# Ordering the second pair of adding transfers behind the last store in a two-branch encoder block

## The chip, the core and the metric

The kernel runs on one NeuronCore of a Trainium2 chip. The metric is the device time of one execution in microseconds (us), lower is better. Three runs of the kernel before gave 907.93, 908.09 and 908.94 us; the median is 908.09 us. The profile belongs to one further execution, of 908.01 us, on which all sums are made.

## The reference

One layer of an encoder block on x of 1024 tokens by 1024 channels, in float32. Cut to what matters here:

```python
h = rmsnorm(x, norm_g)
q, k, v, za, u, vs, zs, gm = split(h @ w_in)
a   = (window_sink_attention(rope(q), rope(k), v, sinks) * silu(za)) @ w_att_out
sgo = (gelu(u) * mix(layernorm(gelu(vs))) * silu(zs)) @ w_sg_out
ga, gs = split(sigmoid(gm + b_merge))
y = ga * a + gs * sgo
out = rmsnorm(x + y @ w_o, final_g)
```

The stretch of the kernel that the change touches begins with the product for za, goes on with the product of s = gelu(u) * mixed * silu(zs) with w_sg_out, and ends with the product of a (attention times silu(za)) with w_att_out.

## The kernel before

**Products.** Every large product is done as a seven-product (Strassen-like) scheme on halves. The right-hand side (the activations, 1024 channels by 1024 tokens) exists as seven "forms", named in the order in which the products use them: b11, t1, t2, b21, t3, b22, t4. Each form is 128 partitions by 4 by 512 numbers and is kept twice: a high part (fp32r, suffix h) and a low part, the rest (suffix l). The high part is a cast or a scaling on ScalarE (L154 for a form with changed sign, L159 without), the low part a subtraction on VectorE (L155, L160); each is made in two halves of 128x1024, so one form is four instructions. The weights (wh, wl) are split in the same two lines, in tiles of 128x1024 or 128x512.

`gemm_pair` (L359 and on) makes two row blocks of the result, with seven products of 12 matmuls each, in the order b11, t1, t2, b21, t3, b22, t4. Between them it empties the accumulators: x11 is copied after b11 (L368), x22 after t1 with changed sign (L372), x12 after t2 (L375), all on ScalarE; x11 += b21's product (L380), x22 -= the accumulator after t3 (L385) and x12 += b22's product (L389) on VectorE. Then `finish` is called for the four quarters in the order x11, x22, x12 and a fourth tile that takes t4's product, called the last quarter below. These x tiles share five buffers, which go round in the order of their first writing. So the copy of x22 in a pair reuses the buffer of x11 of the pair before, and the copy of x12 reuses that of x22: each has to wait until the store of that older tile has read it.

**Stages around the change.** Each stage is four calls of `gemm_pair`:

- The za stage: `finish` applies SiLU (L1670); a hook or more later the tile is multiplied by a tile of the attention result (`times`, L1557 or L1558) and stored to a_dr by a transfer that GpSimd issues (L466). The last pair's four stores are the end of the stage.
- The s stage (product with w_sg_out): `finish` multiplies by a gate (a sigmoid on ScalarE, L1683; the product on VectorE, L1692, or L1690 for the last quarter) and stores to y_dr, again by GpSimd (L466).
- The a stage (product with w_att_out): the same with the other gate, adding into y_dr.

**The forms of s and of a.** `forms_of` (L1510) makes the seven forms from four quarters of 128x4x512, called q11, q12, q22 and minus21, which lie in the four tiles bq0 to bq3. Its steps: q12 = q11 - q12 on VectorE; fill b11 from q11 and t1 from q12; q12 += q22 by a **first pair of adding transfers** (`add_aside`: two transfers of 128x2x512 issued by GpSimd, L202); fill b21 from minus21 and t2 from q12; minus21 += q12 by a **second pair of adding transfers**; q11 = q12 - q11 on VectorE (L190); fill t3 from q11 and b22 from q22. The form t4 is filled from minus21 after the second pair of adding transfers has landed. `last_form` asks for that at the third hook of the next stage's first pair, and its two casts are ordered behind the copy of x12 (`pace[0]`). The first steps happen while the stage before still runs its last pair.

**What sets the order.** Each engine works through its instructions in one order. A planner writes it before the run: it takes instructions by their place in the source as soon as it believes their operands to be ready. `after(second, first)` binds two instructions of one engine to an order without a wait for the first to finish. Transfers issued by GpSimd go through one software queue; those of SyncE (loads, L205) through another; all use the same 16 DMA engines. In what follows add2 means the second pair of adding transfers, with its two halves.

The order that GpSimd had before at the end of the za stage is: add1 first half, add1 second half, add2 first half, store of x11, add2 second half, stores of x22, x12 and the last quarter. At the end of the s stage: add1 (two), store of x11, add2 (two), stores of x22, x12 and the last quarter.

Of the kernel before, what the change touches and what calls it, by code (L numbers as in the profile page):

```python
# [27 lines left out]
ALU = mybir.AluOpType  # L28
# [24 lines left out]
def hybrid_tile(  # L53
# [16 lines left out]
    nc = tc.nc  # L70
# [91 lines left out]
    def after(second, first):  # L162

        tc.add_manual_dep(
            second.ins,
            first.ins.name,
            mybir.DependencyInfo(mybir.DependencyClass.NoSync, mybir.DependencyReason.DATA),
            reason="order",
        )
# [9 lines left out]
    def new_b(names=FORMS):  # L179
        return {n: (slot(n + "h"), slot(n + "l")) for n in names}  # L180

    def fill_b(b, name, src, minus=None):
        hi, lo = b[name]
        minus = name == "t2" if minus is None else minus
        return [
            split(hi[:, c : c + 2, :], lo[:, c : c + 2, :], src[:, c : c + 2, :], minus) for c in range(0, 4, 2)
        ]

    def combine(op, dst, a, c):
        return [op(dst[:, i : i + 2, :], a[:, i : i + 2, :], c[:, i : i + 2, :]) for i in range(0, 4, 2)]  # L190
# [8 lines left out]
    sums_to_make = []  # L199

    def add_to(dst, src):
        nc.gpsimd.dma_start(dst, src, accum_op=ALU.add)  # L202

    def copy_to(dst, src):
        nc.sync.dma_start(dst, src)  # L205
# [34 lines left out]
    def half_of(half):  # L240
        return slice(half * HALF, (half + 1) * HALF)
# [220 lines left out]
    def place(dst, m, half):  # L462
        return dst[m * P : (m + 1) * P, half_of(half)]

    def put(dst, m, half, src, queue=nc.sync):
        queue.dma_start(place(dst, m, half), src)  # L466

    def get(src, m, half, bufs, tag="g"):
        g = mtile([P, HALF], F32, tag, bufs, pool)
# [3 lines left out]
    def rest(dst, m):  # L473


        def finish(i, half, q, src, sign):
            if sign < 0:
                nc.scalar.mul(q[:], src, sign)
            put(dst, m + i, half, q[:])

        return finish
# [37 lines left out]
    for half in range(2):  # L519
        hi, lo = (part[:, half, :] for part in g_parts)  # L520
        src = g_row[:, half_of(half)]
# [40 lines left out]
    def add_on(dst, src):  # L562
        return nc.gpsimd.dma_start(dst, src, accum_op=ALU.add)
# [79 lines left out]
    def w_vs(i, j, c):  # L643
        return w[W_VS + 4 * i + 2 * j + c]

    def two_k(v, c):
        return v[:, 2 * c : 2 * c + 2, :]

    def flat(v):
        return v.rearrange("p k n -> p (k n)")  # L650
# [174 lines left out]
    for c in range(2):  # L825
        move = add_on(flat(two_k(raws["s3"], c)), w_vs(0, 0, c))
# [138 lines left out]
    def mix(g, half, q):  # L965

        pm = bank("tp")
        for t in range(4):
            nc.tensor.matmul(  # L969
                pm[:, t * P : (t + 1) * P],  # L970
                xh[:, half * 4 + t, g * P : (g + 1) * P],
                bias[-1][1][:, g % 4, :],
                start=True,
                stop=True,
            )
        p3 = pm[:].rearrange("p (t i) -> p t i", t=4)
        nc.vector.scalar_tensor_tensor(
            p3,
            p3,
            lg_sb[:, g : g + 1],  # L980
            bias[-1][0][:, g % 4, :].unsqueeze(1).broadcast_to([P, 4, P]),
            op0=ALU.mult,
            op1=ALU.add,
        )
        nc.vector.tensor_mul(q[:], q[:], pm[:])
        put(s1_dr, g, half, q[:])
# [198 lines left out]
    for m in range(0, KC, 2):  # L1185

        def finish(i, half, q, src, sign):
            if sign < 0:
                nc.scalar.mul(q[:], src, sign)
            put(q_raw, m + i, half, q[:])  # L1190
            rows = slice((m + i) * P, (m + i + 1) * P)
            split_q(q[:], [(slice(0, P), q_hl[:, rows, half_of(half)].rearrange("a p t -> p a t"))])

        if m == 2:
            steps_of_q.append(rope_tables())
        if m == 4:
            steps_of_q.append(rotate_keys(0))
            steps_of_q.append(rotate(0, 3))
        gemm_pair(hb, finish, part_of_q)
# [310 lines left out]
    def forms_of(qs, behind_t1=()):  # L1510
        q11, q12, minus21, q22 = (qs[k] for k in QUARTERS)
        b = {}

        def fill(name, q, minus=None):
            b.update(new_b((name,)))
            return fill_b(b, name, q, minus)

        def add_aside(dst, src):
            for i in range(0, 4, 2):
                add_to(dst[:, i : i + 2, :], src[:, i : i + 2, :])  # L1520

        combine(nc.vector.tensor_sub, q12, q11, q12)
        yield
        fill("b11", q11)
        low = fill("t1", q12)[-1]
        for move in behind_t1:
            after(move, low)
        add_aside(q12, q22)
        fill("b21", minus21, True)
        low = fill("t2", q12)[-1]  # L1530
        for hi in hi_of[-2:]:
            after(hi, of_units[-2])
        add_aside(minus21, q12)
        for sub in combine(nc.vector.tensor_sub, q11, q12, q11):
            after(sub, low)
        fill("t3", q11)
        fill("b22", q22)
        yield b
        fill("t4", minus21)
        for hi in hi_of[-2:]:  # L1540
            after(hi, pace[0])
        yield
# [118 lines left out]
    for m in range(0, KC, 2):  # L1661
        if m == 0:
            for _ in range(2):
                want_gate(at_dr, *of_att.pop(0))
        if m == 6:
            s_forms = forms_of(s_q, late_rows)
            next(s_forms)

        def finish(i, half, q, src, sign):
            pace[0] = nc.scalar.activation(q[:], src, AF.Silu, scale=sign)  # L1670
            silus.append((q, m + i, half))

        gemm_pair(hb, finish, lambda: part_of_s(m), "tp")
# [21 lines left out]
    for m in range(0, KC, 2):  # L1695
        if m == 2:
            a_q = {}
            ahead_of_time += loads_of_quarters(a_q, a_dr)
        if m == 6:
            a_forms = forms_of(a_q)  # L1700
            next(a_forms)

        def finish(i, half, q, src, sign):
            gated(q, src, sign, gate_of(gs_dr, m, i, half, KC))
            put(y_dr, m + i, half, q[:], nc.gpsimd)
            want_gate(*((gs_dr, m + 2 + i, half) if m < 6 else (ga_dr, i, half)))

        gemm_pair(sb_, finish, part_of_loads if m else last_form(s_forms, part_of_loads), "tp")
# [65 lines left out]
    for m in range(0, KC, 2):  # L1774
        if m == 6:
            written[0] += 1
            had = [mtile([P, D], F32, "s", 2) for _ in range(2)]
            for i in range(2):
                copy_to(had[i][:], y_dr[(m + i) * P : (m + i + 1) * P, :])

        def finish(i, half, q, src, sign):
            gated(q, src, sign, gate_of(ga_dr, m, i, half, 0))
            if m < 6:
                add_to(place(y_dr, m + i, half), q[:])
                want_gate(ga_dr, m + 2 + i, half)
            else:
                nc.vector.tensor_add(q[:], q[:], had[i][:, half_of(half)])
                if half == 1:
                    last_rows[i] = q
                copy_to(place(y_dr, m + i, half), q[:])  # L1790

        if m == 2:
            ahead_of_time += [lambda name=name: load_o(name, paced) for name in list(O_SOURCES)[:4]]
        hook = lambda: part_of_loads(3)
        gemm_pair(ab, finish, hook if m else last_form(a_forms, hook), "tp")
# [214 lines left out]
```

## Time and profile before

| what | value |
|---|---|
| median of three runs | 908.09 us |
| the profiled execution | 908.01 us |
| its span, first to last instruction | 906.2 us |
| busy time of TensorE (PE) | 893.7 us, 4290 matmuls |
| busy time of VectorE (DVE) | 690.1 us |
| busy time of ScalarE (ACT) | 530.0 us |
| busy time of GpSimd (POOL) | 149.9 us |
| software queue (issued by GpSimd) | 22464 packets, 62.93 MB |
| hardware queue (issued by SyncE) | 110072 packets, 149.74 MB |

A row of the timeline gives the start and the length in us, the engine, the line of the kernel, the operation, the tile written and the tiles read, the count, and in brackets how long the engine had been idle and what ended it. A row of the chain of waits gives start, length and what the time went to. A row of the windows view gives a stretch, its length, the busy time of each engine with its count of instructions, the granted share of the TensorE clock, the mean busy share of the 16 DMA engines and what they moved. GpSimd's rows for transfers are the time of issuing; the transfer itself ends at its landing, which the view of a tile gives as the time from issue to landing.

### The profile page before, as it was taken

The numbers are of one execution on the slowest core, as the hardware profiler recorded it, in microseconds if no ns is written. First come the engines' busy times: TensorE is split into PE (matmuls) and PEld (weight loads), VectorE is DVE, ScalarE is ACT, GpSimd is POOL, SyncE is SP. The second block draws the span as 40 slices with busy tenths as digits, with TensorE's granted clock in tenths as the row PEclk, the third lists the DMA queues.
The fourth block names the chain that finished last, engine by engine and source line by source line (L and its number), as shares of the span: only waits on it lengthen the run. The fifth ranks groups of instructions, "written<-read, shape, count | busy, mean of one in ns | idle before, by whom it ended". The sixth has DMA issues, their size and how long they took to land.

```text
span 906.2 us, 13224 instructions
## 1 busy us (share of the span) xinstructions
PE 893.7 (99%) x4290; PEld 746.1 (82%) x4290; DVE 690.1 (76%) x1256; ACT 530.0 (58%) x1061; POOL 149.9 (17%) x213
## 2 busy tenths in 40 slices
PE   9999999999999999999999999999999999999996
PEld 6888888888888888888888888888878887888885
DVE  6869966666686778887878888647796488479996
ACT  7866533334445567767677676664675375367443
POOL 2322222203030001111111011201111121110012
PEclk9999999999999999999999999999999999999999
DMA  9997888858778768788786779899899688998632
GB/s 330 208 256 209 263 204 178 169 155 267 254 247 296 209 179 216 209 178 204 171 229 220 241 233 239 211 329 356 310 284 378 220 235 240 305 292 269 208 118 114
DMA packets 132750, 213.77 MB, mean 236 GB/s; under 512 B 12777, under 2 KB 61161, under 8 KB 132682
## 3 DMA queue, kind: packets, MB, share of 16 engines
q1 hardware_dynamic: 110072, 149.74, 49.9%
q0 software_dynamic: 22464, 62.93, 31.1%
q8 instruction: 34, 0.56, 0.3%
q14 instruction: 34, 0.28, 0.1%
q10 hardware_dynamic: 146, 0.27, 0.1%
HBM read 147.74 MB, written 86.11 MB: 258 GB/s over the span
## 4 chain that ended last, share of the span: by engine, by line
PE 87%; issue 5%; DMA 5%; POOL 1%; DVE 1%; ACT 1%; POOLq 0%; DVEq 0%; ACTq 0%
PE ps_mm L350 36%; PE ps_o L350 27%; PE ps_sc L1294 3%; PE ps_mm L707 3%; PE ps_o L707 2%; PE ps_tp L707 2%; PE ps_o L1379 2%; PE ps_sc L350 2%; PE ps_tp L1338 2%; PE ps_tp L350 2%; DMA bq<-bq 2%; PE ps_tp L969 2%; DMA a_dr<-x 1%; PE ps_sc L707 1%; DMA y_dr<-x 1%
## 5 line engine op out<-in xcount | busy, mean ns | idle before, releaser
L159 ACT CAST wh<-s 128x1024 fp32r<-128x1024 f32 (+1 forms) x79 | 79.3, 1006 | 89.8 <-PE ps_mm L350 42.7
L160 DVE TENSOR_TENSOR wl<-wr,wh 128x512 fp32r<-128x512 f32 (+1 forms) x77 | 72.1, 938 | 53.2 <-ACT wh L159 52.2
L160 DVE TENSOR_TENSOR wl<-s,wh 128x1024 fp32r<-128x1024 f32 (+1 forms) x79 | 93.0, 1178 | 11.6 <-ACT wh L159 11.5
L159 ACT CAST wh<-wr 128x512 fp32r<-128x512 f32 (+1 forms) x77 | 63.1, 821 | 59.3 <-PE ps_mm L350 33.0
L350 PE MATMUL ps_o<-T_t1h,wh 128*128 128x512 f32 x148 | 58.6, 396 | 0.0
L350 PE MATMUL ps_mm<-T_t3h,wh 128*128 128x512 f32 x140 | 55.6, 397 | 2.8 <-ACT x L375 2.8
L350 PE MATMUL ps_o<-T_b22h,wh 128*128 128x512 f32 x148 | 58.3, 394 | 0.0
L350 PE MATMUL ps_o<-T_t1h,wl 128*128 128x512 f32 x148 | 57.8, 391 | 0.0
L350 PE MATMUL ps_o<-T_b22l,wh 128*128 128x512 f32 x148 | 57.8, 390 | 0.0
L350 PE MATMUL ps_o<-T_b22h,wl 128*128 128x512 f32 x148 | 57.7, 390 | 0.0
L350 PE MATMUL ps_o<-T_t1l,wh 128*128 128x512 f32 x148 | 57.6, 390 | 0.0
L1307 ACT ACTIVATE pr<-ps_sc,sm 128x192 f32<-128x192 f32 (+2 forms) x128 | 50.9, 410 | 8.8 <-DVE sm L1303 6.3
L350 PE MATMUL ps_mm<-T_t3h,wl 128*128 128x512 f32 x140 | 55.4, 395 | 0.0
L350 PE MATMUL ps_mm<-T_t3l,wh 128*128 128x512 f32 x140 | 55.2, 394 | 0.0
L350 PE MATMUL ps_mm<-T_t4h,wh 128*128 128x512 f32 x140 | 55.0, 393 | 0.0
L350 PE MATMUL ps_mm<-T_b11h,wh 128*128 128x512 f32 x140 | 54.9, 392 | 0.0
L350 PE MATMUL ps_mm<-T_t4h,wl 128*128 128x512 f32 x140 | 54.7, 391 | 0.0
L350 PE MATMUL ps_mm<-T_b11l,wh 128*128 128x512 f32 x140 | 54.7, 391 | 0.0
L350 PE MATMUL ps_mm<-T_b11h,wl 128*128 128x512 f32 x140 | 54.6, 390 | 0.0
L350 PE MATMUL ps_mm<-T_t2h,wl 128*128 128x512 f32 x140 | 54.6, 390 | 0.0
L350 PE MATMUL ps_mm<-T_t2h,wh 128*128 128x512 f32 x140 | 54.6, 390 | 0.0
L350 PE MATMUL ps_mm<-T_t2l,wh 128*128 128x512 f32 x140 | 54.6, 390 | 0.0
(399 smaller groups left out, 2402.6 us busy)
## 6 DMA issues: line engine op xcount, KB each, us to landing
wr<-in_w_dram SPq DMA_DIRECT2D x86, 256.0 KB
sums<-in_w_dram POOLq DMA_DIRECT2D x20, 512.0 KB, 6.7
s<-sums SPq DMA_DIRECT2D x20, 512.0 KB
q_hl<-qhl SPq DMA_DIRECT2D x16, 512.0 KB
q<-q_hl SPq DMA_DIRECT2D x64, 128.0 KB
y_dr<-x POOLq DMA_DIRECT2D x28, 256.0 KB, 6.8
g<-in_w_dram POOLq DMA_DIRECT2D x12, 512.0 KB, 7.0
wr<-in_w_dram SPq DMA_DIRECT2D x11, 512.0 KB
```

Of the source, the lines that this page charges most:

```text
L159: hi_of.append(nc.scalar.copy(hi, src))
L160: return nc.vector.tensor_sub(lo, src, hi.bitcast(F32))
L350: nc.tensor.matmul(acc, lt, rt, start=fresh and k == 0 and n == 0, stop=k == 3 and n == 2, skip_group_check=True,)
L707: mm = nc.tensor.matmul(acc[:], lt, rt, start=fresh and k == 0 and n == 0, stop=k == 3 and n == terms[-1], skip_group_check=True,)
L969: nc.tensor.matmul(pm[:, t * P : (t + 1) * P], xh[:, half * 4 + t, g * P : (g + 1) * P], bias[-1][1][:, g % 4, :], start=True, stop=True,)
L1294: nc.tensor.matmul(sc[:, i, k0:], q_of[:, c, i * P : (i + 1) * P], kt[:, f, k0:], start=f == 0, stop=f == 1,)
L1307: nc.scalar.activation(held_in[c, i], sc[:, i, lo:hi], AF.Exp, bias=nmax[:, c, i : i + 1], scale=-1.0, accum_out=sums[:, c, i : i + 1],)
L1338: nc.tensor.transpose(dst, pr[:, i, block * P : block * P + width], ident[:])
L1379: nc.tensor.matmul(po[:, cs], lt, rt, start=n == 0, stop=n == len(terms) - 1)
```

## The change

Every store made by `put` is recorded in a list. In `forms_of`, the two transfers of the second adding pair (minus21 += q12) are ordered on GpSimd behind the newest store in that list. For the forms of s that is the store of the last quarter of the za stage to a_dr; for the forms of a it is the store of the last quarter of the s stage to y_dr. Nothing is computed differently, and no other order is given.

```diff
     def add_to(dst, src):
-        nc.gpsimd.dma_start(dst, src, accum_op=ALU.add)
+        return nc.gpsimd.dma_start(dst, src, accum_op=ALU.add)
...
+    stores = []
+
     def put(dst, m, half, src, queue=nc.sync):
-        queue.dma_start(place(dst, m, half), src)
+        stores.append(queue.dma_start(place(dst, m, half), src))
...
         def add_aside(dst, src):
-            for i in range(0, 4, 2):
-                add_to(dst[:, i : i + 2, :], src[:, i : i + 2, :])
+            return [add_to(dst[:, i : i + 2, :], src[:, i : i + 2, :]) for i in range(0, 4, 2)]
...
-        add_aside(minus21, q12)
+        for move in add_aside(minus21, q12):
+            after(move, stores[-1])
         for sub in combine(nc.vector.tensor_sub, q11, q12, q11):
             after(sub, low)
```

## The prediction

> **What bounds the kernel now.** I read the page first, then the timeline of TensorE for gaps, then the chain of waits at each gap, and last the queues behind it.
>
> ```profile
> span 906.2 us, 13224 instructions
> PE 893.7 (99%) x4290; PEld 746.1 (82%) x4290; DVE 690.1 (76%) x1256; ACT 530.0 (58%) x1061; POOL 149.9 (17%) x213
> ```
>
> TensorE is the bound: an order on GpSimd can gain only where TensorE stands still. The timeline of TensorE shows two gaps around the change:
>
> ```profile
> 675.63 0.39 PE L350 MATMUL ps_tp<-T_b21h,wl 128*128 128x512 f32 x1
> 678.28 0.50 PE L350 MATMUL ps_mm<-T_t3h,wh 128*128 128x512 f32 x1 [2.26 <-ACT x L375]
> ...
> 685.47 0.39 PE L350 MATMUL ps_mm<-T_b11h,wh 128*128 128x512 f32 x1
> ...
> 686.60 0.39 PE L350 MATMUL ps_mm<-T_t4h,wh 128*128 128x512 f32 x1
> ...
> 755.96 0.39 PE L350 MATMUL ps_tp<-T_b21h,wl 128*128 128x512 f32 x1
> 756.92 0.50 PE L350 MATMUL ps_mm<-T_t3h,wh 128*128 128x512 f32 x1 [0.57 <-ACT x L375]
> ...
> 763.62 0.39 PE L350 MATMUL ps_mm<-T_t4h,wh 128*128 128x512 f32 x1
> ```
>
> Both stand at the same place: in the first pair of the s stage and of the a stage, ahead of t3, which needs the accumulator that the copy of x12 (L375) empties. Note the order: after t3 and b22 come five matmuls of the next pair's b11 (685.47), and only then t4 (686.60). The chain of waits says what the copy waited for:
>
> ```profile
> 665.90 11.66 DMA a_dr<-x
> ...
> 677.64 0.59 ACT x L375
> ...
> 678.28 4.60 PE ps_mm L350 x12
> ...
> 745.96 10.24 DMA y_dr<-x
> ...
> 762.65 5.44 PE ps_mm L350 x24
> ```
>
> It waited for the store of the old x22, whose buffer it reuses. That store took 11.66 us in one stage, 10.24 in the other. The last row is the undisturbed pace: 24 matmuls in 5.44 us, 2.72 a product. The t3 product at 678.28 took 4.60. The windows view says why, and how full the transfers are:
>
> ```profile
> 675.20:678.60 3.40, 1.14 (x5) 0.65 (x4) 2.40 (x3) 0.96 (x2) 0.00 (x0) 1.00 0.96 377
> 678.60:682.00 3.40, 3.40 (x10) 2.62 (x9) 2.80 (x3) 3.37 (x4) 0.00 (x0) 0.51 0.73 240
> 660.00:679.00 19.00, 16.74 (x73) 13.54 (x72) 17.13 (x19) 12.66 (x17) 3.94 (x6) 0.99 1.02 302
> 741.00:757.00 16.00, 15.43 (x69) 12.48 (x67) 16.00 (x18) 10.22 (x13) 3.35 (x5) 1.00 1.04 296
> ```
>
> After a stretch of 3.4 us in which TensorE was busy for 1.14, its granted clock was 0.51 for the next 3.4 us. And the 16 DMA engines were fully busy (shares 1.02 and 1.04) over the whole time in which stores and adding transfers were under way.
>
> **What goes: the two gaps.** Without its wait, t3 would start 0.23 us after the last matmul of b21, at 675.86, and t4 5.44 + 5 x 0.227 = 6.57 later, at 682.43; it started at 686.60. That is **4.17 us**, 2.4 of standing still and 1.8 of the half clock. In the a stage: 755.96 + 0.23 + 6.57 = 762.76 against 763.62, **0.86 us**. Together 5.03 us, if nothing else is late. Does the wait go? GpSimd's issues, in order:
>
> ```profile
> 655.80 0.87 POOL L202 DMA_DIRECT2D bq<-bq  x1 [0.25 <-DMA g<-at_dr]
> 660.99 0.85 POOL L202 DMA_DIRECT2D bq<-bq  x1 [4.32 <-DVE x L385]
> 661.74 0.68 POOL L466 DMA_DIRECT2D a_dr<-x  x1
> 665.35 0.85 POOL L202 DMA_DIRECT2D bq<-bq  x1 [2.94 <-DVE wl L160]
> 665.90 1.42 POOL L466 DMA_DIRECT2D a_dr<-x  x2
> 667.56 0.55 POOL L466 DMA_DIRECT2D a_dr<-x  x1 [0.23 <-DVE x L1557]
> 685.25 0.54 POOL L466 DMA_DIRECT2D y_dr<-x  x1 [17.14 <-DVE x L1692]
> ...
> 745.42 0.85 POOL L202 DMA_DIRECT2D bq<-bq  x1 [3.15 <-DVE wl L160]
> 745.96 1.96 POOL L466 DMA_DIRECT2D y_dr<-x  x3
> ```
>
> The second half of add2 (665.35) stands on GpSimd ahead of three stores, and both halves are ahead of them in the queue. With the change the store of x22 is issued before 665.35 and has only the store of x11 and the first adding pair ahead in the queue. In the view of the tile: the landings of that pair (issued at 654.67 and 655.80); those of the last store of the za stage (667.56) and of the last two of the s stage (the second and third of the three at 745.96, the third issued at 747.1); and that of the adding transfer that took least, with nothing ahead of it (issued at 735.00):
>
> ```profile
> DMA to landing us min/median/max: 5.8/7.4/9.0
> ```
>
> ```profile
> DMA to landing us min/median/max: 11.7/11.7/11.7
> ...
> DMA to landing us min/median/max: 10.8/11.0/11.1
> ```
>
> ```profile
> DMA to landing us min/median/max: 5.4/5.4/5.4
> ```
>
> The first adding pair is through at 655.80 + 9.0 = 664.8. Behind it the store of x22, half the size of the transfer that took 5.4 us alone, is down by 665.35 + 5.4 = 670.8, and t3 wants its accumulator only at 675.86: the copy of x12 no longer waits. I count the 5.03 us as won at that place.
>
> **What is added: add2 becomes last in the queue.** Its halves are issued after the last store, at 667.56 + 0.55 = 668.1 and about 669.0. Behind them GpSimd was idle for 17.14 us, until the first store of the s stage (685.25), so their wait blocks no issue there. Their landing is the unknown cost. Lower end: nothing in front, 669.0 + 5.4 = 674.4. Upper end: the longest time in the rows, 669.0 + 11.7 = 680.7. I take **679.8**, near the upper end, because of the queue's order and not of a typical time: the six transfers (two adding halves, four stores) are the same and go through in order, the engines were full, and the last of them landed at 667.56 + 11.7 = 679.2. Whichever is last lands about then; now it is the second half of add2, which before was ahead of three stores. To that comes up to 1.3 us in which the queue waits for the last products, half of it counted. In the a stage the last landing was 11.1 us after an issue at 747.1, which is 758.2, and I take **758.9** (758.2 to 759.5).
>
> **Who waits for add2.** Form t4: its casts, and on the in-order engines everything written behind them. ScalarE first, then VectorE:
>
> ```profile
> 678.12 1.99 ACT L159 CAST T_t4h<-bq 128x1024 fp32r<-128x1024 f32 x2
> 680.13 1.28 ACT L1683 ACT_TABLE_LOAD   x1
> 681.43 0.72 ACT L1683 ACTIVATE g<-g,bm_sb 128x512 f32<-128x512 f32 x1
> 682.06 1.03 ACT L159 CAST wh<-wr 128x1024 fp32r<-128x1024 f32 x1
> ...
> 756.76 2.00 ACT L159 CAST T_t4h<-bq 128x1024 fp32r<-128x1024 f32 x2
> ```
>
> ```profile
> 683.12 1.23 DVE L160 TENSOR_TENSOR wl<-wr,wh 128x1024 fp32r<-128x1024 f32 x1 [0.96 <-ACT wh L159]
> 684.87 0.68 DVE L385 TENSOR_TENSOR x<-x,ps_mm 128x512 f32<-128x512 f32 x1
> ...
> 690.93 1.22 DVE L190 TENSOR_TENSOR bq<-bq,bq 128x1024 f32<-128x1024 f32 x1 [2.24 <-DMA bq<-a_dr]
> ...
> 762.45 0.68 DVE L385 TENSOR_TENSOR x<-x,ps_mm 128x512 f32<-128x512 f32 x1
> ```
>
> Behind the second cast of t4 on ScalarE come the table load, the first gate and the cast of the next pair's weights, which its b11 needs; on VectorE behind t4's low parts comes L385, which frees the accumulator that t4 adds into. From the start of the second t4 cast (678.12 + 0.95 = 679.07) to the end of L385 (685.55) went 6.48 us, and t4 started 1.05 later. In the a stage the same is 757.71 to 763.13, 5.42 us. These chains have no idle time worth naming but that for one another, so I move them whole with the landing.
>
> - s stage: second cast at 679.85, L385 done 6.48 later, hand-over 0.1: t4 at 686.43 against 686.60. Of 4.17 us won, 4.0 are given back; 0.17 is left.
> - The half clock: the next weights' cast ends 4.02 us after the second t4 cast starts, at 683.9, the low part at 685.1. TensorE has finished b22 at 681.30 and stands until 683.9, so from 682.0 to 685.4 it is busy for some 0.8 us, less than the 1.14 after which the clock was halved. Of the next 3.4 us t4 gets about 2.4 at half pace: 1.2 lost. Its bounds: 0 and 1.8, which it cost before.
> - a stage: second cast at 758.95, 5.42 and 0.1 later t4 at 764.47 against 763.62: 0.85 us later than before. There TensorE waits only some 1.1 us for the low part of the weights, so no half clock.
>
> The Trainium skill ("TensorE: Matmul & The Clock Gate", section "HAM oscillation — how this bites in real kernels") puts the rule as no idle gaps above about 3.4 us; this case's trace speaks against it, since a gap of 2.4 us brought the half clock. By that rule the new gap would cost nothing more and the sum would be 1.2 us less.
>
> SyncE's first load of a quarter of a goes into the buffer that add2 reads, so it also waits for the landing, 1.5 us longer than before; behind it are two more loads of a. Their reader, L190 at 690.93, already stands 2.24 us, and the work behind it is for t3 of the next pair, 8 us later: counted at nothing; without that cover it would cost up to 1.5.
>
> **The sum.** 908.01 - 0.17 + 1.2 + 0.85 = 909.9, say **910.0 us**. The profiled execution stands 0.1 under the median of the runs, 908.09. With the landings 0.6 us sooner in both stages and no half clock it is 907.5; with 0.7 later, and the half clock at its bound, 912.
>
> **Rivals.**
>
> *The adding transfers land early.* If an adding transfer is held up only by its own length, its 5.4 us decide: landing at 674.4 and, in the a stage, by 755, both before the copy of x12 would have ended. Then t4's casts follow the copy as now and the full 5.03 us are won: **903.0 us**. For it: 5.4 and 5.8 us were seen. Against it: both were at the head of an empty queue, and the DMA share was above 1. It decides from a landing before about 676, each us later giving back one. The Trainium skill ("DMA: Bandwidth & Descriptors", section "Anatomy of one DMA — SWDGE (gpsimd) path") fits such a transfer at 2.0 us plus its bytes over 436 GB/s, an estimate of 3.2 us for 512 KB; by it this rival would hold. The rows above, 5.4 us at best, do not agree.
>
> *The planner turns the order around.* If it believes add2 to land later than the gate's inputs, it writes table load, gate and weight cast ahead of t4's casts. Then nothing but t4 itself waits: its second half needs a cast of 1.04 and a low part of 1.23 us after the landing, so is ready at 682.1, and would be wanted at 682.43 + 1.36. Also **903.0 us**. Against it: before, it held add1 landed within some 6 us (issued to 655.80, add2's first half put at 660.99, ahead of the store of x11), and from 669.0 add2 has as long until the copy of x12. The trace cannot show this order.
>
> *Later still.* Quarters of a, gates and weights load through the same full engines. If the landing slips to 682 and 761, the slip (2.2 and 2.1 us) counts in full, and the half clock goes on: **914 us**. Against it: the bytes ahead of add2 in its own queue are the same as before.
>
> *No effect.* The order of GpSimd's issues is exactly what is bound, so the change does what it says; 908.0 could only come out as a balance.
>
> **How the numbers follow.** Forecast 0.58, the two early cases together 0.27, later still 0.15. About 0.2% (1.8 us) is what a measurement of this kernel can tell from no change. The forecast's own range, 907.5 to 912, lies on both sides of 909.8: 0.35 slower, 0.20 the same, 0.03 faster. Later still is slower; of the early cases 0.26 faster, 0.01 the same. So faster 0.29, same 0.21, slower 0.50. The range for 8 in 10 runs from 902.9, which takes in the early cases, to 912.5.
>
> **What would show it.** In the profile after: GpSimd issues four stores in a row and then both halves of add2; no gap ahead of t3 in either first pair, and the copy of x12 waiting for nothing; instead a gap ahead of the next pair's b11 near 681.3 to 684, ended by the weight cast at L159; t4's second cast starting at a landing near 680 and 759; a stretch at half clock near 685. It is wrong if add2 lands before 677, or if the gate at L1683 stands ahead of t4's casts on ScalarE.

## The result, and the profile after

The kernel after takes 912.92 us (median of six runs, 912.37 to 914.85), against 908.01 us for six runs of the kernel before beside them (905.47 to 908.94). The ratio on record is 1.0075, with a 95% interval of 1.0060 to 1.0091: slower by about 0.75%. The quotient of these two medians is smaller, 1.0054, below that interval; a second measurement (after again, below) gave 1.0081, and 1.0084 by the medians. The forecast was 910.0 us with a range to 912.5. The direction was right, the size too small, and the time lies 0.4 us outside the range. The profiled execution took 912.37 us:

```profile
span 910.6 us, 13223 instructions
```

The timeline of GpSimd shows the order that was meant: four stores, then both halves of add2, and in the a stage the same.

```profile
661.57 0.57 POOL L468 DMA_DIRECT2D a_dr<-x  x1 [5.05 <-DVE x L1559]
...
667.40 0.54 POOL L468 DMA_DIRECT2D a_dr<-x  x1 [1.20 <-DVE x L1559]
668.02 1.79 POOL L202 DMA_DIRECT2D bq<-bq  x2
...
748.30 1.14 POOL L468 DMA_DIRECT2D y_dr<-x  x2 [1.77 <-DVE x L1694]
749.50 1.78 POOL L202 DMA_DIRECT2D bq<-bq  x2
```

The timeline of ScalarE shows what came of it, first for the s stage, then for the a stage:

```profile
673.51 0.58 ACT L375 COPY x<-ps_mm 128x512 f32<-128x512 f32 x1
677.11 1.05 ACT L159 CAST T_t4h<-bq 128x1024 fp32r<-128x1024 f32 x1 [3.02 <-DMA bq<-bq]
680.33 1.05 ACT L159 CAST T_t4h<-bq 128x1024 fp32r<-128x1024 f32 x1 [2.17 <-DMA bq<-bq]
...
683.31 1.03 ACT L159 CAST wh<-wr 128x1024 fp32r<-128x1024 f32 x1
...
759.37 1.05 ACT L159 CAST T_t4h<-bq 128x1024 fp32r<-128x1024 f32 x1 [2.57 <-DMA bq<-bq]
762.67 1.05 ACT L159 CAST T_t4h<-bq 128x1024 fp32r<-128x1024 f32 x1 [2.25 <-DMA bq<-bq]
```

The copy of x12 (L375) has no bracket any more: it waits for nothing. The wait now stands in front of the two casts of t4, and its releaser is add2. The next pair's weights are cast only at 683.31, behind t4's second cast, the table load and a gate. The timeline of TensorE follows:

```profile
675.69 0.39 PE L350 MATMUL ps_mm<-T_t3h,wh 128*128 128x512 f32 x1
...
684.39 0.79 PE L350 MATMUL ps_mm<-T_b11h,wh 128*128 128x512 f32 x1 [3.10 <-ACT wh L159]
...
687.10 0.63 PE L350 MATMUL ps_mm<-T_t4h,wh 128*128 128x512 f32 x1
...
691.51 0.39 PE L350 MATMUL ps_mm<-T_b11h,wl 128*128 128x512 f32 x1
...
693.12 0.39 PE L350 MATMUL ps_o<-T_t1h,wh 128*128 128x512 f32 x1
...
758.40 0.39 PE L350 MATMUL ps_mm<-T_t3h,wh 128*128 128x512 f32 x1
...
765.33 0.50 PE L350 MATMUL ps_mm<-T_b11h,wh 128*128 128x512 f32 x1 [1.33 <-ACT wh L159]
...
767.96 0.50 PE L350 MATMUL ps_mm<-T_t4h,wh 128*128 128x512 f32 x1 [0.23 <-DVE x L385]
...
772.41 0.39 PE L350 MATMUL ps_o<-T_t1h,wh 128*128 128x512 f32 x1
```

The gap ahead of t3 is gone in both stages. The new gap stands ahead of the next pair's b11, 3.10 us in the s stage, and t4's twelve matmuls take 691.51 - 687.10 = 4.41 us. The windows view of the same stretch (busy times of the engines, then granted clock, share of the transfer engines and GB/s) says why:

```profile
680.42:683.83 3.41, 0.87 (x4) 0.38 (x2) 1.82 (x2) 3.38 (x4) 0.00 (x0) 1.00 0.68 181
683.83:687.24 3.41, 2.80 (x6) 1.72 (x7) 2.87 (x4) 3.30 (x5) 0.58 (x1) 0.50 1.05 397
687.24:690.65 3.41, 3.41 (x10) 2.64 (x9) 2.50 (x4) 0.00 (x0) 1.09 (x2) 0.50 0.97 333
```

The clock stood at one half for 6.8 us, twice the stretch that was forecast.

**One measure for both stages.** From t3 of the first pair to t1 of the second stand 48 matmuls (t3, b22, t4 and the next b11), 48 x 0.2267 = 10.88 us at full pace. What lies above that is the loss of a stage; where t3 itself waits, the count begins at the end of b21. The kernel before had t1 here:

```profile
690.91 0.39 PE L350 MATMUL ps_o<-T_t1h,wh 128*128 128x512 f32 x1
...
767.93 0.39 PE L350 MATMUL ps_o<-T_t1h,wh 128*128 128x512 f32 x1
```

Before: 690.91 - 675.86 - 10.88 = 4.17 us lost in the s stage and 767.93 - 756.19 - 10.88 = 0.86 in the a stage. After: 693.12 - 675.69 - 10.88 = 6.55 and 772.41 - 758.40 - 10.88 = 3.13. The sum went from 5.03 to 9.68, up by 4.65, and the profiled execution from 908.01 to 912.37, up by 4.36. So, to within 0.3 us, the whole of the difference lies in these two places.

All kernels by this measure (us; the losses come from each one's profiled execution; medians of 4 to 12 runs, one for the last row; in the two kernels with the gap filled, the loss in s includes the 5.9 us of the filling matmuls):

| kernel | lost in s | lost in a | profiled | median | ratio to before (95%) |
|---|---|---|---|---|---|
| before | 4.17 | 0.86 | 908.01 | 908.01 | |
| after | 6.55 | 3.13 | 912.37 | 912.92 | 1.0075 (1.0060 to 1.0091) |
| order in the s stage alone | 6.26 | 0.97 | 908.66 | 909.10 | 1.0040 (1.0025 to 1.0055) |
| order in the a stage alone | 0.94 | 3.39 | 907.24 | 908.94 | 1.0028 (1.0012 to 1.0044) |
| behind the store of x22 | 1.59 | 0.00 | 904.76 | 905.29 | 0.9987 (0.9976 to 0.9999) |
| after, weights early | 4.21 | 2.54 | 910.42 | 910.10 | 1.0047 (1.0031 to 1.0063) |
| before, weights early | 0.63 | 0.88 | 904.39 | 906.68 | 1.0009 (0.9994 to 1.0024) |
| after, fewer loads | 1.88 | 0.00 | 904.41 | 905.61 | 1.0003 (0.9991 to 1.0014) |
| after, gap filled | 5.90 | 4.34 | 920.89 | 920.83 | 1.0175 (1.0157 to 1.0193) |
| after, gap filled, second try | 6.04 | 3.46 | 910.28 | 912.94 | 1.0070 (1.0044 to 1.0096) |
| behind x22, weights early | 0.13 | 0.13 | 903.17 | 903.28 | 0.9973 (0.9960 to 0.9987) |
| after again | 6.53 | 3.37 | 913.11 | 913.21 | 1.0081 (1.0057 to 1.0105) |
| before again | 3.18 | 0.98 | 907.26 | 907.26 | |

Beside the later kernels the kernel before had medians of 906.08, 905.58 and 905.59 us (31, 29 and 11 runs, 902.88 to 909.28 in all). So ratios are compared below, not times.

### The profile page after: what moved, and what is told of

It is laid out like the page before. It is cut to its first block, busy times and chain, and to the rows that moved or that the text cites. A ratio compares the mean times of both kernels' runs of the same rounds, so it can differ in the third digit from the quotient of the medians.

```text
span 910.6 us, 13223 instructions
## 1 busy us (share of the span) xinstructions
PE 895.5 (98%) x4290; PEld 745.8 (82%) x4290; DVE 689.8 (76%) x1256; ACT 529.6 (58%) x1061; POOL 149.8 (16%) x213
## 4 chain that ended last, share of the span: by engine, by line
PE 77%; issue 13%; DMA 5%; POOL 2%; ACT 1%; DVE 1%; SPq 0%; POOLq 0%; ACTq 0%; DVEq 0%
PE ps_mm L350 31%; PE ps_o L350 24%; PE ps_sc L1296 3%; DMA bq<-bq 3%; PE ps_mm L709 2%; PE ps_o L709 2%; PE ps_tp L709 2%; PE ps_sc L350 2%; PE ps_o L1381 2%; PE ps_tp L1340 2%; PE ps_tp L971 2%; PE ps_sc L709 1%; DMA g<-at_dr 1%; PE ps_sc L593 1%; PE ps_tp L350 1%
## 5 line engine op out<-in xcount | busy, mean ns | idle before, releaser
L350 PE MATMUL ps_mm<-T_t4l,wh 128*128 128x512 f32 x140 | 55.2, 395 | 0.0
```

What stands on the lines that cost most here:

```text
L350: nc.tensor.matmul(acc, lt, rt, start=fresh and k == 0 and n == 0, stop=k == 3 and n == 2, skip_group_check=True,)
```

## The experiments

**Each stage alone.** One of the two calls gets the order of before.

```diff
-    def forms_of(qs, behind_t1=()):
+    def forms_of(qs, behind_t1=(), bound=True):
...
         for move in add_aside(minus21, q12):
-            after(move, stores[-1])
+            if bound:
+                after(move, stores[-1])
...
-            a_forms = forms_of(a_q)
+            a_forms = forms_of(a_q, bound=False)
```

The other kernel has `bound=False` in the call for the forms of s.

> The order stands for the forms of s alone; those of a have the order of before. If each stage pays for its own wait (the chain behind t4's casts moves with the landing of add2), the time is that of before plus what t4 lost in the s stage, 693.12 - 690.91 = 2.2 us: 908.0 + 2.2 = 910.2 us, the stretch of 6.8 us at half clock after 683.8 is there again, and the a stage has its gap ahead of t3 back. Rival: the s stage's loss is won back by slack later on, and the whole change comes from the a stage: 908.0.

> The order stands for the forms of a alone. If each stage pays for its own wait, the time is 908.0 + 2.3 = 910.3 us (the a stage's part of the 4.48 us by which the next pair's t1 came later in the kernel after), with the gap of 2.3 us and the half clock of before in the s stage, and the second half of add2 landing some 2.3 us later against the last products than the queue's end did before. Rival: 908.0, or 912.4 if it is the a stage alone.

Each is slower by itself, by 0.40% and 0.28%; the sum, 0.68%, lies within the interval of both together. Each stage pays for itself. One part of the first expectation missed: with the order in the s stage alone the half clock lasted 3.41 us (684.55 to 687.96) and not 6.8, although the gap ahead of b11 was longer, 3.64 us. The kernel with the order in the a stage alone showed something else in the s stage, where it has the order of before. Its ScalarE there:

```profile
675.34 0.59 ACT L375 COPY x<-ps_mm 128x512 f32<-128x512 f32 x1 [1.21 <-DMA a_dr<-x]
```

The store of the old x22 let the copy go at 675.34, where the profile of before had 677.64, and t3 hardly waited (0.05 us): this execution lost 0.94 us in the s stage, not 4.17.

**Before and after once more.** The same two kernels again.

> The kernel after once more, beside the kernel before on the same chip. If the losses of the two stages add up, the ratio is that of the order in the s stage alone plus that in the a stage alone, 1.0040 + 0.0028: 1.007, and the trace again has t1 of the second pair 17.4 us behind t3 in the s stage and 14.0 in the a stage (10.9 without a wait). If they don't, the ratio is nearer to one of the two alone, 1.003 to 1.004.

> The kernel before once more. The first profile of it had lost 4.2 us in the s stage (t3 to the next t1 15.1 us from the end of b21, against 10.9 without a wait), 1.8 of them to the half clock. If that is what every execution loses, it is seen again. If the wait for the store varies from execution to execution and passes into the half clock only where it is long, as the s stage of the kernel with the order in the a stage alone suggests (0.9 us lost, no half clock), this one may show less, and its time then is lower by the same amount: 905 us with a loss of 1 us.

After again has a ratio of 1.0081, losses of 6.53 and 3.37, and so adds up as expected. Before again lost 3.18 us in the s stage, with nearly the wait of the first profile and yet without the half clock (0.9 of the 3.18 lie behind t3, where b11 and t4 wait). TensorE, and the windows view:

```profile
678.09 0.50 PE L350 MATMUL ps_mm<-T_t3h,wh 128*128 128x512 f32 x1 [2.13 <-ACT x L375]
```

```profile
673.40:676.81 3.41, 2.56 (x12) 1.79 (x10) 3.41 (x4) 0.99 (x2) 0.00 (x0) 1.00 1.01 365
676.81:680.22 3.41, 2.13 (x9) 1.79 (x10) 1.46 (x3) 2.75 (x4) 0.00 (x0) 1.00 0.66 210
```

The boundaries of the two stretches are the times at which this trace's own clock can change (the last section says how that is read from the traces). The wait lies across such a boundary, so that TensorE was busy for 2.56 and 2.13 us of 3.41; in the first profile nearly the same wait lay within one stretch, of which 1.14 us were busy, and the half clock followed.

So what the kernel before loses in the s stage differs from execution to execution (4.17, 3.18, 0.94 and 0.63 us in four profiles that have its order there), by the landing of one store and by whether the half clock follows. The loss in the a stage hardly differs (0.86 to 0.98).

**What stands behind t4's casts.** The next pair's weights are split ahead of t4's casts and of the gates, in the first pair of both stages.

```diff
         pace[0] = nc.scalar.copy(x12[:], acc)
         split_next()
+        if soon:
+            split_next()
         hook()
...
         finish(0, 0, x11, x11[:], 1.0)
-        split_next()
+        if not soon:
+            split_next()
...
             after(hi, pace[0])
+            after(hi, of_units[-1])
...
         after(gate, pace[0])
+        if m == 0:
+            after(gate, of_units[-1])
```

> The change as it is, and in the first pair of the s and of the a stage the next pair's weights are cast and split ahead of t4's casts and ahead of the gates. Nothing is taken from add2's wait. Theory (the loss comes from what is queued behind t4's casts on ScalarE and VectorE, not from t4 itself): next b11 follows b22 without a gap, no half clock in the s stage, and t4 starts when the second low part (landing + 1.05 + 1.23) and L385 (0.7 more) are done, near 683.4 in place of 687.1 and about 765.7 in place of 768.0: 912.4 - 3.7 - 1.7 - 2.3 = 904.7 us. Rival (the landing of add2 itself is what t4 waits for, with the rest hidden): 911 to 912.5 us.

> The kernel before, with the next pair's weights cast and split ahead of t4's casts and of the gates in the first pair of the s and the a stage. Theory (in the kernel before, the copy of x12 is what TensorE waits for, and t4's casts are off the path): same as the kernel before within 0.5 us. Rival (the chain behind t4's casts costs time in the kernel before too): 2 us faster.

On the kernel before it changes nothing that can be told (1.0009, with 1 in the interval). On the kernel after it takes the ratio from 1.0075 to 1.0047, 2.5 us and not the 7.7 expected. ScalarE, VectorE and TensorE of that kernel, and two windows of each stage:

```profile
676.21 1.06 ACT L159 CAST wh<-wr 128x1024 fp32r<-128x1024 f32 x1 [1.57 <-PE ps_tp L350]
...
680.96 1.05 ACT L159 CAST T_t4h<-bq 128x1024 fp32r<-128x1024 f32 x1 [2.24 <-DMA bq<-bq]
```

```profile
682.04 1.23 DVE L160 TENSOR_TENSOR T_t4l<-bq,T_t4h 128x1024 fp32r<-128x1024 f32 x1 [2.07 <-ACT T_t4h L159]
...
683.78 0.68 DVE L388 TENSOR_TENSOR x<-x,ps_mm 128x512 f32<-128x512 f32 x1
```

```profile
684.60 0.47 PE L350 MATMUL ps_mm<-T_t4h,wh 128*128 128x512 f32 x1 [2.31 <-DVE x L388]
...
764.95 0.47 PE L350 MATMUL ps_mm<-T_t4h,wh 128*128 128x512 f32 x1 [2.29 <-DVE x L388]
```

```profile
681.95:685.36 3.41, 1.10 (x5) 0.67 (x4) 3.32 (x5) 3.38 (x6) 0.00 (x0) 1.00 0.96 292
685.36:688.77 3.41, 3.41 (x9) 2.65 (x8) 2.71 (x4) 1.47 (x2) 1.54 (x3) 0.50 1.05 373
...
760.46:763.87 3.41, 2.20 (x10) 1.50 (x8) 1.49 (x2) 2.57 (x4) 0.00 (x0) 1.00 0.58 204
763.87:767.28 3.41, 2.33 (x10) 1.99 (x11) 3.41 (x6) 1.89 (x3) 1.58 (x2) 1.00 0.20 70
```

The theory holds for the weights: they are cast at 676.21, and the gap ahead of b11 is gone. But t4 itself still waits, 2.3 us in each stage, for L385 (here L388), which stands with L380 (here L382) behind t4's low parts on VectorE. The chain from the landing to t4 became 684.60 - 680.96 = 3.64 us in place of 687.10 - 680.33 = 6.77. The wait passes into the half clock in the s stage (685.36) and not in the a stage, and the planner now puts two matmuls of b11 ahead of t4 where five stood, which takes 0.7 us of cover away in each stage. So both theories were partly right: the chain shrank by nearly half, but of the 9.68 us lost only 2.9 went (6.75 are left), and for the rest t4 still waits on the landing.

**The half clock.** 26 matmuls into a bank that nobody reads fill the gap of the s stage.

```diff
         product(t5, ready[n, 5], b["b22"], False)
+        if idle:
+            spare = bank("sc")[:]
+            for i in range(idle):
+                nc.tensor.matmul(spare, ready[n, 5][0][:, 0:P], b["b22"][0][:, 0, :], ...)
```

> The change as it is, with 26 matmuls of 128x512 into a spare bank behind b22 of the s stage's first pair (5.9 us of work that nobody reads), so that TensorE is busy until t4 is ready at 687.1. The five matmuls of the next b11 then come behind t4 and not ahead of it. Theory (half of what the s stage lost behind t4's start is the half clock, 1.7 us): no half clock after 683.8, t4's product takes 2.72 us and not 4.41, and the next t1 starts at 687.1 + 5.44 = 692.6, 0.5 us sooner than after although b11's five matmuls have moved behind. Rival (t4's 4.41 us have another cause, such as operands read while they are written): t4 still takes 4.4 us and the next t1 starts 1.1 us later than in the kernel after.

The ratio is 1.0175, 9 us more than after, and that is another wait, behind the place that was to be measured. VectorE of that kernel:

```profile
696.98 1.23 DVE L190 TENSOR_TENSOR bq<-bq,bq 128x1024 f32<-128x1024 f32 x1 [7.65 <-DMA bq<-a_dr]
```

The planner had put the difference for the forms of a (L190), which waits for a load, ahead of the low part of the next weights, and TensorE stood 5.4 us behind both. The second try binds that difference behind the second pair's L380:

```diff
-        combine(nc.vector.tensor_sub, q12, q11, q12)
+        for sub in combine(nc.vector.tensor_sub, q12, q11, q12):
+            if held:
+                after(sub, held[0])
```

> The change as it is with the 26 matmuls into a spare bank behind b22 of the s stage's first pair, and the difference of quarters for the forms of a (L190), on which the first try of this stood 5.8 us, ordered behind the b21 sum of the second pair, near where the kernel after has it. Theory (1.7 us of the s stage's loss is the half clock): t4's product takes 2.72 us at full clock, the next t1 starts 0.5 us sooner than in the kernel after although five matmuls of b11 have moved behind t4, and the time is 0.5 us below that of the kernel after. Rival (t4's 4.41 us have another cause): t4 takes 4.4 us, and the time is 1 us above the kernel after.

Its t3, t4 and t1 on TensorE, and the windows view:

```profile
673.76 0.39 PE L350 MATMUL ps_mm<-T_t3h,wh 128*128 128x512 f32 x1
...
685.15 0.47 PE L350 MATMUL ps_mm<-T_t4h,wh 128*128 128x512 f32 x1
...
690.68 0.39 PE L350 MATMUL ps_o<-T_t1h,wh 128*128 128x512 f32 x1
```

```profile
681.80:685.20 3.40, 3.40 (x17) 2.61 (x15) 2.62 (x4) 2.60 (x4) 0.49 (x1) 1.00 1.05 401
685.20:688.60 3.40, 3.40 (x16) 2.84 (x16) 3.18 (x5) 1.72 (x2) 1.18 (x3) 1.00 0.99 343
```

t4 starts 685.15 - 673.76 = 11.39 us behind t3, as in the kernel after (687.10 - 675.69 = 11.41). The clock stays at 1.00, and t4 and the next b11 take 690.68 - 685.15 = 5.53 us for 24 matmuls, where the kernel after took 693.12 - 687.10 = 6.02 for 19 (at full pace 4.31). So the half clock cost 1.7 us behind t4's start, and the rival is out: the same operands at full clock give the full pace. The time (1.0070) can't be told from that of after (1.0081); the 0.5 us expected is too little to be told.

**Why add2 lands so late.** The loads of summed weight blocks are left out where they run beside add2.

```diff
+            if 26 <= n <= 30:
+                sa = sb = r0
-            for a, dst in enumerate((sa, sb)):
+            for a, dst in enumerate(() if sa is r0 else (sa, sb)):
                 copy_to(
```

> The change as it is, but the loads of the sums of weight blocks (two of 512 KB a pair) are left out for five pairs, the four of the s stage and the first two of the a stage as far as they have such loads; those products take a tile that is there anyway, so the output is not the layer's. Theory (an adding transfer moves as fast as the loads of SyncE leave the 16 engines to it): with two 512-KB loads fewer beside it, the second half of add2 lands 2 to 3 us sooner in the s stage and about 3 us sooner in the a stage, and t4 and all behind it follow: some 5 us below the kernel after, 907 to 908 us. Rival (the software queue has its own pace, and what lies ahead in it sets the landing): landings and time as in the kernel after, a ratio to the kernel before of 1.0075.

ScalarE of that kernel:

```profile
676.30 1.05 ACT L159 CAST T_t4h<-bq 128x1024 fp32r<-128x1024 f32 x1 [2.22 <-DMA bq<-bq]
...
753.51 1.05 ACT L159 CAST T_t4h<-bq 128x1024 fp32r<-128x1024 f32 x1 [1.60 <-DMA bq<-bq]
```

The second half of add2 releases its cast at 676.30, 1.8 us behind t3 (674.51 here), where the kernel after had 680.33 - 675.69 = 4.6; in the a stage 753.51 - 752.55 = 1.0 against 762.67 - 758.40 = 4.3. So it lands 2.8 and 3.3 us sooner with the same transfers ahead of it in the same queue. The ratio falls to 1.0003. That is more than was expected: the s stage still waits a little, but no longer long enough for the half clock, and the a stage not at all.

The view of the queues shows that the loads set the pace, but that the transfers met no more of them in the s stage than before the change. A row gives a queue (q0 is the software queue, q1 that of SyncE), its packets, the MB moved and its share of the 16 engines' time. In each kernel the last 2.10 MB of the software queue in the s stage are the four stores and the two halves of add2. Here is the stretch in which they move: before (665.3 to 678.7), after (666.4 to 679.9), and after with fewer loads (664.5 to 675.8):

```profile
q0 software_dynamic: 607, 2.10, 59.1%
q1 hardware_dynamic: 1141, 2.14, 43.3%
...
q0 software_dynamic: 607, 2.10, 58.2%
q1 hardware_dynamic: 1037, 1.93, 40.8%
...
q0 software_dynamic: 608, 2.10, 70.0%
q1 hardware_dynamic: 590, 1.06, 25.0%
```

With 1.06 MB of loads beside it in place of 1.93, the queue takes 11.3 us and not 13.5. But from before to after the pace is the same (13.4 and 13.5 us) and the loads are no more; the queue only began 1.1 us later. Until then it had nothing under way: from 664.18 to 665.32 before, from 663.92 to 666.45 after. Its rows for 664.0 to 666.4, before and after:

```profile
q0 software_dynamic: 39, 0.15, 31.6%
...
q0 software_dynamic: 1, 0.00, 0.0%
```

In these 2.4 us SyncE's loads had shares of 74.9% and 104.0%. What stood next in the queue had been issued long before: the first half of add2 at 660.99 before, the store of x11 at 661.57 after. The profiles of after again, of weights early and of the second gap-filled kernel have the same 2.5 us. With the order in the s stage alone it was otherwise: there the queue was empty for 0.6 us only, but took 15.2 us for the 2.10 MB, and t4's second cast started 5.2 us behind t3. In the a stage the queue moved add1's second half, add2 and the four stores, 2.62 MB, in 16.9 us before, of which it stood empty for 0.8; after, it needed 19.1 us and stood empty for 2.3 (the longest stretch is 749.99 to 751.97). Why transfers that have been issued start so late, and what divides the delay into an empty and a slow queue, no run shows.

**A better place.** add2 behind the store of x22, the one store for which the copy of x12 waits; then the same with the weights early.

```diff
-            after(move, stores[-1])
+            after(move, stores[-3])
```

> add2 is ordered behind the store of x22, the second of the four, and not behind the last; the stores of x12 and of the last quarter follow add2. Theory (the software queue goes through its transfers in order, so what stands ahead is what counts): the copy of x12 no longer waits, since the old x22 is stored ahead of add2, and add2 lands about as it did before, its second half near 675 to 677 and 755 to 757, by when t4's casts would start anyway: both gaps go, 5.0 us are won, 903 us. Rival (transfers share the full engines whatever their order in the queue, so add2 lands near 680 and 760 in any place): t4's casts still wait, 911 to 912 us.

> add2 behind the store of x22, and the next pair's weights ahead of t4's casts and of the gates. With add2 behind the store of x22 the s stage still lost 1.6 us (to the cast of the weights behind t4's second cast, and t4), the a stage nothing. Theory: that goes too, so 1.6 us below add2 behind x22 alone, a ratio to the kernel before of 0.997. Rival (t4's own wait for the landing at 677.2 is what is left): no difference from add2 behind x22 alone, 0.9987.

Behind the store of x22 alone the ratio is 0.9987. ScalarE and TensorE of that kernel in the s stage:

```profile
677.21 1.05 ACT L159 CAST T_t4h<-bq 128x1024 fp32r<-128x1024 f32 x1 [2.14 <-DMA bq<-bq]
```

```profile
683.75 0.50 PE L350 MATMUL ps_mm<-T_t4h,wh 128*128 128x512 f32 x1 [0.24 <-DVE x L385]
```

Neither t3 nor, in the a stage, t4 waits. In the s stage add2 lands at 677.2, at the late end of what was expected, and so the rival (near 680 in any place) is out: the place in the queue counts too. But that was not in time: 1.59 us are lost behind t4's second cast. With the weights early as well both stages lose 0.13 us, and the ratio is 0.9973 (0.9960 to 0.9987), 1.3 us below the place alone (by the difference of the ratios, 0.0014 x 906; the two intervals overlap, so that this step is not certain). This version beats both kernels: its interval lies below 1 throughout. That removing what the profile of before had lost, 5.03 us, brings only 0.27%, about 2.5 us, agrees with the smaller loss that other executions of the kernel before had.

## Why the prediction was right in kind and short in size

**What bounds, what goes: right.** The two gaps ahead of t3 are gone, and the copy of x12 waits for nothing. The 5.03 us belong to the profiled execution of before; other executions lose less in the s stage (0.63 to 3.18 us). This raised the measured ratio, since the kernel before is mostly faster than its first profile (71 later runs have a median of 905.8 us), but it does not explain why the kernel after took more than 910.0.

**The rivals: "early", "planner" and "no effect" are out.** The second half of add2 landed near 680.3, and the gate stands behind t4's casts, ahead of the weights' cast at 683.31.

**Who waits for add2: right, to within 0.3 us.** From t4's second cast to t4 it takes 687.10 - 680.33 = 6.77 us in the s stage (forecast 6.58 with the hand-over) and 767.96 - 762.67 = 5.29 in the a stage (forecast 5.52). SyncE's loads of a, which wait for the same landing, were counted at nothing: from t4's start in the s stage to the a stage TensorE has no gap that shows them.

**The landing: this step failed.** The prediction took that "Whichever is last lands about then", and added up to 1.3 us in which the queue waits, half of it counted. By the start of t3, without its wait, the second half was expected at 679.8 - 675.86 = 3.9 us in the s stage and 758.9 - 756.19 = 2.7 in the a stage. It was there at 4.6 and 4.3, so 0.7 and 1.6 us later, and in the a stage beyond the bound of 759.5 (3.3 us). "The engines were full" was true and beside the point: they were full of SyncE's loads while the software queue stood empty. The mis-sized term is that empty time. In the s stage it grew from 1.1 to 2.5 us, and the 2.10 MB behind it moved as fast as before, so all of the 1.3 us came and not half. (With the order in the s stage alone the same delay came as slower moving.) In the a stage the queue needed 2.3 us more in all; it stood empty for 1.5 of them, and for 0.8 it moved more slowly. That quarters, gates and weights load through the same engines was named under the rival "later still", at 0.15. The a stage's loss, 2.27 us above before, lies nearer to that rival (0.85 + 2.1 = 2.95) than to the forecast (0.85), but of the delay in that stage only 0.8 us is slower moving beside the loads, as that rival had it. That leaving out loads moves the landing by 2.8 and 3.3 us shows what the loads cost in this kernel, not what the change added.

**The half clock: right in kind, short in size.** Forecast one stretch of 3.4 us and 1.2 us lost, bound 1.8; it was two stretches and 1.7 us. The forecast put the boundaries of the stretches at 682.0 and 685.4, as the trace of before had them; in the trace after they are 680.42, 683.83 and 687.24. In the stretch from 683.83 b11 began late, TensorE was busy for 2.80 us of 3.41 (second row of the first windows view), and the half clock went on through the next stretch, which t4, begun at 687.10, took in full.

**The sum.** Loss expected: 4.17 - 0.17 + 1.2 = 5.2 in the s stage, 0.86 + 0.85 = 1.7 in the a stage, 6.9 together; measured 9.7. The 2.8 us missing are the landing, 0.7 + 1.6, and the half clock, 0.5; the chains, 0.2 too short and 0.2 too long, come out even, which is luck.

## What to carry to other kernels

Moving a transfer to the end of its queue moves a wait, it doesn't remove it: name the reader of what is now last and all that stands behind that reader on its in-order engine, and look for the one place that serves both readers (here behind the second of four stores). The landing of a transfer is not set by its place in its own queue alone, so list what the other queue moves in the same microseconds, and look at each queue's own share: engines that are full can hide a queue that stands empty. And size a stall from several executions: one profile gave 5.0 us where the better version won about 2.5.

## What the runs showed of the hardware

- The clock is granted by stretches of 3.41 us that lie on a grid, and not by the length of a gap. Every trace has a half-clock stretch at its end, and in the six that have more the starts lie whole numbers of 3.413 us apart: with the gap filled (first try) at 699.06, 774.15 and 914.10, which are 22 and 41 such lengths. Divided by that grid, all 13 traces agree behind their first 20 us: at full clock, every stretch in which TensorE was busy for 1.40 us or less was followed by half the clock, and every one with 1.52 or more was not; at half clock, 2.51 and 2.80 us kept it there, and 3.08 and more ended it. The Trainium skill ("TensorE: Matmul & The Clock Gate", section "Part 1: The HAM clock gate (the "warmup" mystery)") describes a free-running activity window of about 3.4 us, so that the phase counts; the traces here agree.
- Gaps of 3.10 and 3.25 us held the clock at one half for 6.8 us, longer ones of 3.64 and 5.43 us only for 3.4, and a gap of 2.3 us for 3.4 or not at all. The Trainium skill ("TensorE: Matmul & The Clock Gate", section "HAM oscillation — how this bites in real kernels") has the rule of no gaps above about 3.4 us; it is too generous for this kernel, and here the measurement decides.
- The two 512-KB adding transfers at the end of the queue release their casts 680.33 - 677.11 = 3.2 and 762.67 - 759.37 = 3.3 us apart. The Trainium skill ("DMA: Bandwidth & Descriptors", section "Anatomy of one DMA — SWDGE (gpsimd) path") gives 2.0 us plus bytes over 436 GB/s, an estimate of 3.2 us for one transfer from issue to landing: that agrees neither with the 5.4 us of the quickest one, alone, nor with the 12 us from the second one's issue (668.60) to its landing, most of which it spent behind others. That the spacing comes out near it is no test of it.
- The software queue can stand empty with transfers issued: 2.5 us in the s stage after (663.92 to 666.45) behind a store issued at 661.57, while the share of the 16 engines was full.
